# Layer 0's latent stage: its narrow transposes emitted one at a time behind every third wide matmul

## The chip, the cores and the metric

The kernel runs on one core of a Trainium2 chip. The metric is the device time of one execution in microseconds (us); the time of a kernel is the median of its runs.

TensorE (PE in the profile) multiplies matrices and also transposes 128x128 blocks, as a product with an identity matrix; VectorE (DVE), ScalarE (ACT) and GpSimd (POOL) do the elementwise work; SyncE (SP) issues most DMA transfers. Each engine takes its instructions in the order of its own queue, so an instruction that waits holds up all those behind it on that engine. The order in each queue is fixed when the kernel is built: the framework schedules with a simulated timeline and keeps the order edges that the program adds.

## The reference, cut to what matters

A two-layer backbone over 2048 latent rows and 256 context rows of width 1024. Layer 0 (even) computes, from the modulated rows `h`, query and key/value latents, the heads of a latent attention, and the inputs of a gated linear attention:

```python
h = rms_norm(x, norm_g[i]) * (1 + scale) + shift
lat = split_cols(jnp.dot(h, w_in), EVEN_SPLITS)          # lat[0]: 768, lat[1]: 256, lat[2]: 32 columns
...
q = jnp.dot(rms_norm(q_lat, q_norm), w_uq).reshape(bsz, n, A_HEADS, A_QK)
kv = jnp.dot(rms_norm(kv_lat, kv_norm), w_ukv).reshape(bsz, n, A_HEADS, A_NOPE + A_V)
k = jnp.concatenate(
    [kv[..., :A_NOPE], jnp.broadcast_to(k_rope[:, :, None, :], (bsz, n, A_HEADS, A_ROPE))], axis=-1)
q = rms_norm(q, q_gain)
k = rms_norm(k, k_gain)
...
q = jnp.concatenate([q[..., :A_NOPE], apply_axial_rope(q[..., A_NOPE:], cos, sin)], axis=-1)
```

Everything is float32. The kernel splits each factor of a product into a high and a low half and sums three products (high x high, high x low, low x high). The latent stage makes q, k and v of all rows and writes them to DRAM; the attention that follows reads them back.

## The kernel before

The stage is `even_latent` (lines 393 to 590). Its 2304 rows are 18 tiles of 128 (`NT` is 18; tiles 0 and 1 are context). For each tile:

1. *Rows.* `prep` (line 314) loads the tile from DRAM into `x`, which has one buffer (line 322). ACT squares it with an accumulated sum, `rpow` makes the factor `ssx`, and DVE scales `x` in place (line 328). TensorE transposes it in 8 blocks (line 331) into two PSUM buffers `px` of four blocks each. `modulate` then has ACT apply scale and shift from `modA` and `modB` back into `x`, and splits the result into the halves `hhi` and `hlo` (two buffers each); the modulated rows are stored to `H` by a DMA that ACT issues.
2. *Row products.* `gemm` multiplies them with the weights W0, W1, W2 of 352 columns each, 24 products a weight (8 blocks of depth, three half-products each), 72 in all, in the PSUM tiles `gm`. ACT copies each result into the latent tile `u`; `scaled` normalizes it.
3. *Latents.* `up` (line 487) transposes `u` in 8 blocks into two PSUM tiles `tp` (line 495), splits them into `lth` (ACT) and `ltl` (DVE, line 498), one buffer each, and multiplies: 36 query products of 384 columns with `WU`, into `up` tiles, then 12 key/value products of 512 columns with `wkv`. The values go through `vn` (one buffer) to DRAM. Then come the norms and the rotary embedding that make `qn` and `kn`.
4. *Heads.* `fin` (line 541) transposes the queries and then the keys, 8 heads each, in four groups of four into `tp` tiles (line 549). ACT and DVE scale and split each group into `qkhl` (two buffers, line 553), and SP stores it to `QT` or `KT`.

So a tile has 120 wide products and 32 transposes. `px`, `tp`, `gm` and `up` have two PSUM buffers each, all eight banks. The modulation of later layers (`ada_steps`) is spread over the loop: its scale-and-shift rows end in small transposes that also take `tp` buffers.

The loop (lines 571 to 590) runs steps `s` from 0 to 19. Step `s` emits, in this order: the rows of tile `s+1`, the row products of tile `s`, one step of the modulation, `up` of tile `s-1`, `fin` of tile `s-2`. In each of these the transposes are emitted in one go, 8, or 4 and 4, and the scheduler may move them against products that do not depend on them. From step 17 on, `rest_steps` loads and splits further weights (`w_rest`), and `first` (line 559) computes the last two tiles' row products with two of them, in steps 18 and 19; its result passes through the buffer of `vn`. All three-fold products go through `mm3` (line 114). Every ACT operation has line 106, that of the helper `act`.

The next stage begins with the products `mx` (line 651), which read back the stored queries as `mq` and the keys as `mk`.

Of the kernel before, what the change touches and what calls it, by code (L numbers as in the profile page):

```python
# [10 lines left out]
F32 = mybir.dt.float32  # L11
F32R = mybir.dt.float32r
AF = mybir.ActivationFunctionType
ALU = mybir.AluOpType
# [74 lines left out]
class Kern:  # L89
    def __init__(self, tc, nc, ins, scr):  # L90
        self.tc, self.nc, self.i, self.scr = tc, nc, ins, scr
        self.n = 0
        self.ahead, self.calls, self.chain = [], 0, None

# [19 lines left out]
    def mm3(self, out, lhs, rhs, ks, start=True, stop=True):  # L114

        lh, ll = lhs
        rh, rl = rhs
        n = len(ks)
        for j, k in enumerate(ks):
            self.nc.tensor.matmul(out, lh(k), rh(k), start=start and j == 0, stop=False)  # L120
            self.nc.tensor.matmul(out, lh(k), rl(k), start=False, stop=False)
            self.nc.tensor.matmul(out, ll(k), rh(k), start=False, stop=stop and j == n - 1)

    def mm3_steps(self, out, lhs, rhs, ks):
        lh, ll = lhs
        rh, rl = rhs
        n = len(ks)
        for j, k in enumerate(ks):
            self.nc.tensor.matmul(out, lh(k), rh(k), start=j == 0, stop=False)  # L129
            self.nc.tensor.matmul(out, lh(k), rl(k), start=False, stop=False)  # L130
            yield self.nc.tensor.matmul(out, ll(k), rh(k), start=False, stop=j == n - 1)  # L131
# [185 lines left out]

    def transposed(self, t, src, pp, tag, xp=None):

        nc, sp = self.nc, self.prp  # L320
        x = self.tl(xp or sp, [P, D], "x", bufs=1)
        self.xload = nc.sync.dma_start(x[:], src[t * P : t * P + P, :])
        hi = self.tl(sp, [P, KD, P], "hhi", F32R, bufs=self.hbufs)
        lo = self.tl(sp, [P, KD, P], "hlo", F32R, bufs=self.hbufs)
        ss = self.tl(sp, [P, 2], "ssx")
        self.act(lo[:].rearrange("p k t -> p (k t)"), x[:], AF.Square, accum_out=ss[:, 0:1])
        self.rpow(ss[:, 1:2], ss[:, 0:1], 1.0 / D, EPS)
        nc.vector.tensor_scalar(out=x[:], in0=x[:], scalar1=ss[:, 1:2], scalar2=None, op0=ALU.mult)
        ps = [self.tl(pp, [P, 4, P], tag[0], bufs=tag[1]) for _ in range(2)]
        for k in range(KD):  # L330
            nc.tensor.transpose(ps[k // 4][:, k % 4, :], x[:, k * P : k * P + P], self.ident[:])
        return x, ps, hi, lo
# [60 lines left out]
    def even_latent(self, ws, wrest, kept):  # L393
# [5 lines left out]
        with ExitStack() as es:  # L399
# [87 lines left out]
            def up(t):  # L487
                u, ss = lat.pop(t)
                lh = self.tl(sp, [P, 8, P], "lth", F32R, bufs=1)
                ll = self.tl(sp, [P, 8, P], "ltl", F32R, bufs=1)  # L490
                for g in range(2):
                    ps = self.tl(pp, [P, 4, P], "tp")
                    for j in range(4):
                        k = g * 4 + j
                        nc.tensor.transpose(ps[:, j, :], u[:, k * P : k * P + P], self.ident[:])
                    s = slice(g * 4, g * 4 + 4)
                    self.act(lh[:, s, :], ps[:])
                    nc.vector.tensor_tensor(out=ll[:, s, :], in0=ps[:], in1=lh[:, s, :], op=ALU.subtract)
# [43 lines left out]
            def fin(t):  # L542
                qn, kn = nat.pop(t)
                for z, (src, dst) in enumerate(((qn, self.QT), (kn, self.KT))):
                    col = 2 * z + (0 if t < NCT else 1)
                    for h2 in range(2):
                        ps = self.tl(pp, [P, 4, P], "tp")
                        for j in range(4):
                            nc.tensor.transpose(ps[:A_QK, j, :], src[:, h2 * 4 + j, :], self.ident[:])
                        hl = self.tl(sp, [P, 4, 2, P], "qkhl", F32R, bufs=2)  # L550
                        hi, lo = hl[:A_QK, :, 0, :], hl[:A_QK, :, 1, :]
                        self.act(hi, ps[:A_QK], AF.Copy, scale=qkg[:A_QK, col : col + 1])
                        nc.vector.scalar_tensor_tensor(out=lo, in0=ps[:A_QK], scalar=qkg[:A_QK, col : col + 1],
                                                       in1=hi, op0=ALU.mult, op1=ALU.subtract)
                        nc.sync.dma_start(
                            dst[h2 * 4 : h2 * 4 + 4, :, :A_QK, t * P : t * P + P].rearrange("h s d t -> d (h s) t"),
                            hl[:A_QK].rearrange("d h s t -> d (h s) t").bitcast(F32))
# [12 lines left out]
            ahead = (_ for j in (2, 3, 4) for _ in self.rest_steps(wrest, j, ws, f"W{j - 2}"))  # L570
            for s in range(NT + 2):
# [1121 lines left out]
```

## Time and profile before

| | |
|---|---|
| median of 3 runs | 3750.93 us (3749.34 to 3751.32) |
| the profiled execution | span 3751.7 us |
| mean granted TensorE clock over the span | 0.973 |
| latent stage, first W1 product to first `mx` | 45.2 to 568.4 us |
| wide and narrow products of TensorE in this stretch | 2880 |
| DMA in this stretch | 82.7 MB, mean 158 GB/s |

The whole span, cut into the start, the latent stage, and three stretches of what follows (the attention, the gated linear attention, and the rest with layer 1), shows where the work lies. Columns: the stretch, busy time and count of each engine (PEld is TensorE's weight load, which overlaps its products), TensorE's granted clock as a share of full speed, the mean busy share of the 16 DMA engines, and their rate.

```profile
core 0: us, PE busy (x) PEld busy (x) DVE busy (x) ACT busy (x) POOL busy (x), PEclk, DMA share, GB/s
0.00:45.20 45.20, 33.05 (x160) 20.79 (x160) 14.31 (x29) 18.55 (x36) 3.86 (x17) 0.92 0.82 310
45.20:568.40 523.20, 489.37 (x2880) 452.64 (x2880) 348.33 (x634) 263.13 (x608) 180.90 (x326) 0.96 0.54 158
568.40:1000.00 431.60, 429.76 (x2212) 379.41 (x2213) 351.43 (x591) 59.35 (x103) 42.44 (x73) 1.00 0.26 81
1000.00:1700.00 700.00, 690.56 (x3471) 458.80 (x3469) 503.43 (x735) 337.67 (x665) 135.86 (x136) 0.99 0.32 90
1700.00:3751.00 2051.00, 1944.33 (x9686) 1460.76 (x9684) 1158.22 (x2873) 759.14 (x1329) 843.72 (x784) 0.97 0.54 155
```

How to read the lines of the next part: a row of the timeline gives start, busy time, engine and line, operation, out<-in by the program's names, the shapes, and the count of like instructions run together; in square brackets stands the wait ahead of it and what ended it. Instructions overlap in TensorE's pipeline, so the time from one start to the next (a slot) is what a product costs, not its busy time.

### The profile page before, as it was taken

The page shows a single profiled execution, that of the slowest core. Times are in us where ns is not written, and L with a number is a line of the kernel's source. Part 1 is how long each engine was busy: PE and PEld are TensorE (multiplying, and loading weights), DVE is VectorE, ACT ScalarE, POOL GpSimd, SP SyncE. Part 2 cuts the span into 40 slices and gives each one's busy share as a digit, 9 for nine tenths or more (in the row PEclk, how much of TensorE's full clock was granted, in tenths as well). Part 3 has the DMA queues.
Part 4 walks back from the last instruction along what each step waited for, and adds up shares of the span by engine and source line. Part 5 has one row for each costly group of instructions (what it writes and reads, how often), then busy time and mean ns, then how long its engine had stood idle before and what let it go on. Part 6 is the DMA issues. An engine that isn't in the chain of part 4 may idle for free.

```text
span 3751.7 us, 51747 instructions
## 1 busy us (share of the span) xinstructions
PE 3587.1 (96%) x18404; PEld 2772.4 (74%) x18404; DVE 2375.7 (63%) x4860; ACT 1437.8 (38%) x2741; POOL 1206.8 (32%) x1336
## 2 busy tenths in 40 slices
PE   7999989999999999999999999999899999898889
PEld 6988988888886666656657878887688886555567
DVE  4677656888866666696754344455578774666722
ACT  4445541111125555545552134444222224444400
POOL 1434320010111222212202233333444435776643
PEclk9999999999999999999999999999999999999899
DMA  7455453222252231425515545545544448777464
GB/s 254 138 161 162 130 168 96 80 81 80 77 134 66 75 108 57 117 82 149 143 37 180 162 141 155 148 146 166 178 138 147 127 114 225 188 183 201 140 194 131
DMA packets 364371, 512.18 MB, mean 137 GB/s; under 512 B 25825, under 2 KB 243889, under 8 KB 358210
## 3 DMA queue, kind: packets, MB, share of 16 engines
q1 hardware_dynamic: 322642, 425.49, 39.5%
q0 software_dynamic: 19872, 55.92, 4.9%
q10 hardware_dynamic: 21600, 27.46, 2.1%
q8 instruction: 146, 2.39, 0.3%
q14 instruction: 111, 0.91, 0.1%
HBM read 329.38 MB, written 179.37 MB: 136 GB/s over the span
## 4 chain that ended last, share of the span: by engine, by line
PE 78%; DVE 8%; DMA 6%; POOL 4%; ACT 3%; issue 2%; SPq 0%; POOLq 0%; DVEq 0%; ACTq 0%
PE gm L129 9%; PE gm L130 9%; PE gm L131 9%; PE av L905 7%; PE st L963 4%; PE mx L651 4%; PE st L964 3%; PE st L965 3%; PE pj L129 3%; PE pj L130 3%; PE pj L131 3%; POOL oacc L1409 2%; PE o L1403 1%; DMA wraw<-w_od 1%; PE st L1373 1%
## 5 line engine op out<-in xcount | busy, mean ns | idle before, releaser
L954 DVE TENSOR_TENSOR acc<-acc,apt 128x512 f32<-128x512 f32 x512 | 364.6, 737 | 155.3 <-ACT apt L106 152.3
L106 ACT ACTIVATE apt<-st 128x512 f32<-128x512 f32 (+1 forms) x592 | 343.9, 593 | 282.5 <-PE st L965 245.3
L652 DVE TENSOR_REDUCE mm<-mx 128x1 f32<-128x512 f32 (+1 forms) x656 | 389.2, 629 | 82.1 <-PE mx L651 75.1
L905 PE MATMUL av<-apt,av 128*64 128x512 f32 (+1 forms) x1184 | 286.2, 597 | 0.0
L963 PE MATMUL st<-aq,akh 97*128 97x512 f32 (+1 forms) x592 | 254.0, 429 | 5.8 <-ACT apt L106 3.0
L1409 POOL TENSOR_TENSOR oacc<-oacc,opt 128x576 f32<-128x576 f32 (+6 forms) x192 | 221.4, 1178 | 87.0 <-ACT opt L106 85.3
L651 PE MATMUL mx<-mk,mq 96*128 96x512 f32 (+1 forms) x656 | 236.8, 373 | 6.1 <-DMA mq<-QT 4.7
L964 PE MATMUL st<-aq,akh 96*128 96x512 f32 (+1 forms) x592 | 235.1, 397 | 0.0
L965 PE MATMUL st<-aq,akl 96*128 96x512 f32 (+1 forms) x592 | 234.0, 396 | 0.0
L1286 DVE CUSTOM_DVE_ANT_1 mx<-mx,mtab 128x225 f32<-128x225 f32 (+12 forms) x576 | 183.8, 339 | 61.4 <-PE mx L1280 45.9
L106 ACT ACTIVATE u<-gm 128x352 f32<-128x352 f32 (+1 forms) x140 | 68.5, 497 | 369.8 <-PE gm L131 208.8
L905 PEld LDWEIGHTS av<-apt,av 128*64 128x64 f32 x1184 | 81.6, 137 | 155.3 <-issue 154.1
L1531 DVE TENSOR_TENSOR opt<-st,tab 128x64 f32<-128x64 f32 (+10 forms) x576 | 142.5, 314 | 78.7 <-PE st L1374 50.8
L963 PEld LDWEIGHTS st<-aq,akh 97*128 97x128 f32 x592 | 112.4, 190 | 98.9 <-issue 43.7
L1073 POOL TENSOR_TENSOR px<-py,px 128x512 f32<-128x512 f32 x64 | 86.2, 1348 | 231.5 <-DVE py L1072 220.4
L106 ACT ACTIVATE opt<-opt 128x930 f32<-128x930 f32 (+8 forms) x130 | 104.4, 805 | 138.1 <-DVE opt L1531 129.3
L1373 PE MATMUL st<-q,kt 128*128 128x480 f32 (+5 forms) x256 | 104.3, 409 | 47.2 <-DVE opt L1531 42.5
L651 PEld LDWEIGHTS mx<-mk,mq 96*128 96x128 f32 x656 | 121.7, 189 | 17.7 <-issue 5.1
L106 ACT ACTIVATE prh<-pr 128x1024 fp32r<-128x1024 f32 x32 | 33.9, 1058 | 263.4 <-PE pj L130 235.7
L965 PEld LDWEIGHTS st<-aq,akl 96*128 96x128 f32 x592 | 113.5, 192 | 25.5
L964 PEld LDWEIGHTS st<-aq,akh 96*128 96x128 f32 x592 | 114.1, 193 | 18.0
L106 ACT ACTIVATE x<-px,modB,modA 128x128 f32<-128x128 f32 x272 | 99.1, 468 | 57.9 <-DVE onat L1139 27.6
(513 smaller groups left out, 10054.6 us busy)
## 6 DMA issues: line engine op xcount, KB each, us to landing
q<-Q SPq DMA_DIRECT2D x48, 512.0 KB
H<-x ACTq DMA_DIRECT2D x36, 512.0 KB
adaw<-ada_w SPq DMA_DIRECT2D x64, 256.0 KB
x<-H SPq DMA_DIRECT2D x32, 512.0 KB
pr<-RT SPq DMA_DIRECT2D x32, 512.0 KB
wraw<-w_od SPq DMA_DIRECT2D x64, 256.0 KB
K1t<-okt POOLq DMA_DIRECT2D x32, 512.0 KB, 7.7
kt<-K1t SPq DMA_DIRECT2D x32, 512.0 KB
```

Source lines behind the costliest of these rows:

```text
L106: return self.nc.scalar.activation(out, in_, func, **kw)
L129: self.nc.tensor.matmul(out, lh(k), rh(k), start=j == 0, stop=False)
L130: self.nc.tensor.matmul(out, lh(k), rl(k), start=False, stop=False)
L131: yield self.nc.tensor.matmul(out, ll(k), rh(k), start=False, stop=j == n - 1)
L651: mm = nc.tensor.matmul(ps[:, :w], q[:A_QK, (t % 6) * P : (t % 6) * P + P], k[:A_QK, k0 : k0 + w], start=True, stop=True)
L652: nc.vector.tensor_reduce(out=m[:, t, n : n + 1], in_=ps[:, :w], axis=AX.X, op=ALU.max)
L905: nc.tensor.matmul(O[j, nb][i * 64 : i * 64 + 64, :w], V[j, kt // TT][:, kt % TT, i * 64 : i * 64 + 64], pts[i][:, :w], start=n == 0, stop ...
L954: nc.vector.tensor_tensor(out=acc[i][:, :w], in0=a[:, :w], in1=pts[i][:, :w], op=ALU.add)
L963: nc.tensor.matmul(ps[:, :w], kh[: A_QK + 1, i, kq], qh[: A_QK + 1, :w], start=True, stop=False)
L964: nc.tensor.matmul(ps[:, :w], kh[:A_QK, i, kq], ql[:A_QK, :w], start=False, stop=False)
L965: mm = nc.tensor.matmul(ps[:, :w], kl[:A_QK, i, kq], qh[:A_QK, :w], start=False, stop=True)
L1409: self.psum = nc.gpsimd.tensor_tensor(out=a, in0=a, in1=pts[:, :, a0 - r0 : a1 - r0, :], op=ALU.add)
```

## The change

In this stage alone, transposes are no longer emitted as a batch. Each group becomes a generator, one transpose at a time, with the work on a finished PSUM tile (modulation, split or store) emitted behind the last transpose of the group: behind the 4th of four, or, for rows, behind the 8th. `queue` puts such a generator in a list. The new `mm` emits one wide product; it then takes the first generator in the list whose count is due, emits its next transpose with an order edge behind this product, and puts an order edge from that transpose to the next wide product (`hold`). A generator is due again three wide products later. `finish_task` emits all that is left of a generator at once.

```diff
+    def queue(self, gen, wait=0, every=3):
+        task = [self.wide + wait, every, gen]
+        self.narrow.append(task)
+        return task
...
+    def finish_task(self, task):
+        if task in self.narrow:
+            self.narrow.remove(task)
+        for _ in task[2]:
+            pass
+
+    def mm(self, out, l, r, start, stop):
+        with self.tc.issue_after(self.hold.ins) if self.hold else ExitStack():
+            mm = self.nc.tensor.matmul(out, l, r, start=start, stop=stop)
+        self.hold = None
+        self.wide += 1
+        for task in self.narrow:
+            if task[0] <= self.wide:
+                with self.tc.issue_after(mm.ins):
+                    self.hold = next(task[2], None)
+                if self.hold is None:
+                    self.narrow.remove(task)
+                task[0] = self.wide + task[1]
+                break
+        return mm
...
+    def transposes(self, ps, parts, src, done):
+        for n, i in enumerate(parts):
+            t = self.nc.tensor.transpose(ps(i), src(i), self.ident[:])
+            if n == len(parts) - 1:
+                done()
+            yield t
...
+    def prep_task(self, l, t, src, pp, tag, wait):
+        x, hi, lo = self.scaled(t, src)
+        def steps():
+            ps = []
+            for g in range(2):
+                ps.append(self.tl(pp, [P, 4, P], tag[0], bufs=tag[1]))
+                done = (lambda: self.modulate(l, t, x, ps, hi, lo)) if g else lambda: None
+                yield from self.transposes(lambda k: ps[g][:, k, :], range(4), lambda k: x[:, (g * 4 + k) * P : (g * 4 + k + 1) * P], done)
+        return hi, lo, self.queue(steps(), wait)
```

`transposed` and `scaled` are the two parts of the former `transposed`. The latents' transposes leave `up` and become the generator `turn`, with the split of each four behind its fourth; `fin` becomes a generator, with the split and the store of each group behind its fourth. The loop queues the rows of tile `s+1` with a wait of 10 wide products, the latents of tile `s-1` with a wait of 40, and the queries and keys of tile `s-2` with a wait of 2, the last ahead of the products of `up(s-1)`, not behind them:

```diff
             for s in range(NT + 2):
                 if 0 < s < NT - 1:
                     with tc.issue_after(behind.ins) if s == 1 else ExitStack():
-                        hT[s + 1] = self.prep(0, s + 1, self.i["xin"], pp, px)
+                        *hT[s + 1], tasks["x", s + 1] = self.prep_task(0, s + 1, self.i["xin"], pp, px, 10)
+                if 1 < s <= NT:
+                    tasks["u", s - 1] = self.queue(turn(s - 1), 40 if s < NT else 0)
                 if s == 0:
                     gemm(0, 1)
                 elif 1 < s < NT:
+                    begin(("x", s))
                     gemm(s)
...
-                for f, d in ((up, 1), (fin, 2)):
-                    if s >= NT - 1:
-                        for _ in zip(range(3), ahead):
-                            pass
-                        if f == fin and s >= NT:
-                            first(NT - 1, s - NT + 2)
-                            first(NT - 2, s - NT + 2)
-                    if 0 <= s - d < NT:
-                        f(s - d)
+                if s >= NT - 1:
+                    for _ in zip(range(3), ahead):
+                        pass
+                if 0 <= s - 1 < NT:
+                    if s == 1:
+                        tasks["u", 0] = self.queue(turn(0))
+                    begin(("u", s - 1))
+                    if 0 <= s - 2:
+                        tasks["q", s - 2] = self.queue(fin(s - 2), 2)
+                    up(s - 1)
+                if s >= NT - 1:
+                    for _ in zip(range(3), ahead):
+                        pass
+                if s >= NT:
+                    if s > NT:
+                        tasks["q", s - 2] = self.queue(fin(s - 2), 2)
+                    first(NT - 1, s - NT + 2)
+                    first(NT - 2, s - NT + 2)
+                begin(("q", s - 2))
+            self.finish_tasks()
```

`begin` calls `finish_task` for a task that has not run dry. So what is left of the rows of tile `s` is emitted ahead of its row products, and what is left of its latents ahead of its query products. Other stages call `mm3` too; there the list is empty, and `mm` adds no order edge. The text of these stages is unchanged.

More of the change, by code (lines that the diff above doesn't have):

```diff
@@ L93, in __init__ @@
         self.ahead, self.calls, self.chain = [], 0, None
+        self.narrow, self.wide, self.hold = [], 0, None
     def pool(self, es, name, bufs=1, space=None, **kw):
@@ L112, in load, with finish_tasks, mm3 @@
         return self.chain
[L114 to L122, printed above, removed]
+    def queue(self, gen, wait=0, every=3):
+        task = [self.wide + wait, every, gen]
+        self.narrow.append(task)
+        return task
+    def finish_tasks(self):
+        while self.narrow:
+            self.finish_task(self.narrow[0])
+    def finish_task(self, task):
[17 more added lines that the diff above has]
+        return mm
+    def mm3(self, *a):
+        for _ in self.mm3_steps(*a):
+            pass
     def mm3_steps(self, out, lhs, rhs, ks):
@@ L328, in transposed @@
         nc.vector.tensor_scalar(out=x[:], in0=x[:], scalar1=ss[:, 1:2], scalar2=None, op0=ALU.mult)
[L329 to L332, printed above, removed]
+        return x, hi, lo
     def modulate(self, l, t, x, ps, hi, lo):
```

53 lines of the change are left out of this document (33 added, 20 removed).

## Prediction

> **What bounds the kernel now.** I read the page first, then the busy time by stretch of layer 0's latent stage, which the change is confined to, then TensorE's waits in each stretch, then single instructions.
>
> ```profile
> span 3751.7 us, 51747 instructions
> ...
> PE 3587.1 (96%) x18404; PEld 2772.4 (74%) x18404; DVE 2375.7 (63%) x4860; ACT 1437.8 (38%) x2741; POOL 1206.8 (32%) x1336
> ```
>
> TensorE is busy 96% of the span, so what the kernel can gain by a new order is what TensorE loses. The stage runs from the first W1 product at 45.2 us to the first product of the next stage at 568.4. I cut it into a head (tiles 0 to 2), sixteen regular tiles, and a tail after the last tile's row product:
>
> ```profile
> core 0: us, PE busy (x) PEld busy (x) DVE busy (x) ACT busy (x) POOL busy (x), PEclk, DMA share, GB/s
> 45.20:100.00 54.80, 47.19 (x252) 44.73 (x253) 34.82 (x53) 28.00 (x62) 11.79 (x19) 0.88 0.62 194
> 100.00:491.50 391.50, 383.51 (x2309) 353.60 (x2308) 275.97 (x519) 204.98 (x493) 150.94 (x282) 0.99 0.51 149
> 491.50:568.40 76.90, 58.66 (x323) 54.31 (x321) 37.54 (x64) 30.14 (x53) 18.17 (x27) 0.89 0.64 181
> ```
>
> TensorE's loss is its idle time and its time at a lowered clock (1 minus PEclk, times the length). Head: 7.6 + 6.6 = 14.2 us. Middle: 8.0 + 3.9 = 11.9. Tail: 18.2 + 8.5 = 26.7. Together 53 us, 1.4% of the span: no order of the same instructions gains more here. The waits behind the idle time, in the same three stretches:
>
> ```profile
> PE px L331 <- DVE x L328: 2.7, 1, 2.7
> PE up L122 <- DVE ltl L498: 2.7, 1, 2.7
> PE up L120 <- ACT lth L106: 1.1, 1, 1.1
> ```
> ```profile
> PE up L122 <- DVE ltl L498: 3.8, 5, 1.7
> PE tp L495 <- DVE modA L302: 1.9, 1, 1.9
> PE tp L549 <- DVE qkhl L553: 1.5, 2, 1.2
> PE px L331 <- DVE x L328: 0.4, 1, 0.4
> ```
> ```profile
> PE gm L120 <- ACT vn L106: 5.9, 1, 5.9
> PE mx L651 <- DMA mq<-QT: 4.7, 1, 4.7
> PE tp L495 <- DVE qkhl L553: 4.4, 2, 3.5
> ```
>
> Each row is total, times, longest. The middle is nearly tight: five waits for the low half of the latents (ltl) are half of its idle time. Head and tail hold the large ones.
>
> **The change part by part.** No instruction is added or removed: the same 16,410 TensorE instructions, 560 of them transposes of this stage, and the same DMAs, in another order. 534 transposes now stand alone between wide products. *Price of a single.* Four in a batch, and one alone:
>
> ```profile
> 139.06 0.32 PE L121 MATMUL gm<-W0l,hhi 128*128 128x352 f32 x1
> 139.22 0.60 PE L549 MATMUL tp<-ident,kn 128*96 128x128 f32 x4
> 139.58 0.41 PE L122 MATMUL gm<-W0h,hlo 128*128 128x352 f32 x1
> 139.82 0.32 PE L120 MATMUL gm<-W0h,hhi 128*128 128x352 f32 x1
> ```
> ```profile
> 246.20 0.34 PE L121 MATMUL up<-WUl,lth 128*128 128x384 f32 x1
> 246.38 0.27 PE L549 MATMUL tp<-ident,qn 128*96 128x128 f32 x1
> 246.41 0.42 PE L122 MATMUL up<-WUh,ltl 128*128 128x384 f32 x1
> 246.67 0.34 PE L120 MATMUL up<-WUh,lth 128*128 128x384 f32 x1
> ```
>
> A row product takes a slot of 0.16 (139.06 to 139.22), a query product 0.18. From 139.06 to 139.82 are 0.76 us; less two slots, four transposes cost 0.44, 0.11 each. The single: 0.47 less two slots of 0.176 is 0.12, equal within the rounding. So standing alone saves nothing and costs 0 to 0.01 each, 0 to +5 us over 534; I take a quarter of that, **+1.3**, since both figures round to 0.11 or 0.12.
>
> The Trainium skill (TensorE: Matmul & The Clock Gate, "Back-to-back issue gap") gives an isolated 128-column matmul 56 ns once warm, and says that weight loads are pulled ahead of running matmuls; by it a single between wide products might cost half of 0.11. The single above does not show it; it is a rival below.
>
> *Head.* Now tile 0's latents are transposed at once behind the W2 products, tile 2's rows singly among tile 0's query products, and tile 3's rows follow after 5 query, 11 row and 12 key products. With a key slot of 0.24,
>
> ```profile
> 136.04 0.40 PE L120 MATMUL up<-wkvh,lth 128*128 128x512 f32 x1
> 136.28 0.39 PE L121 MATMUL up<-wkvl,lth 128*128 128x512 f32 x1
> ```
>
> that is 0.9 + 1.8 + 2.8 = 5.5 us of cover. The rows' tile x has one buffer: modulation must end before the next load, and square, power and scale follow it. Before, that chain took
>
> ```profile
> 63.75 1.97 PE L331 MATMUL px<-ident,x 128*128 128x128 f32 x8 [2.74 <-DVE x L328]
> 65.95 1.97 PE L495 MATMUL tp<-ident,u 128*128 128x128 f32 x8 [0.23 <-DVE u L467]
> ```
> ```profile
> 79.14 0.74 DVE L328 TENSOR_SCALAR x<-x,ssx 128x1024 f32<-128x1024 f32 x1
> ```
> ```profile
> 85.79 1.50 ACT L106 ACTIVATE x<-px,modB,modA 128x128 f32<-128x128 f32 x4 [2.41 <-DMA wraw<-w_rest]
> ```
>
> from 65.7 to 79.9, 14.2 us. With singles the first four modulations (1.5 us) and their split lie ahead of the last transpose, so 1.5 to 2.6 come off: 11.6 to 12.7, against 5.5. A wait of 6 to 7 us for x stands in TensorE's queue with everything behind it, and SP now issues this x load behind two loads of rest weights, up to 2 us more. I take 7, and 2.5 for the clock (waits of 7.6 in this stretch cost 6.6 at lowered clock before). Gone: the two waits for lth and ltl, 3.8, and their clock, about 1.7. Tile 2's eight transposes lay in the wait up to 65.95, which stays, and now take 1.0 of busy time. Head: 7 + 2.5 - 5.5 + 1 = **+5**, bounds 0 (x lands early) to +9.
>
> *Middle.* The latents are now transposed some 40 wide products into the next row product, so at least 11 row products lie between the last of them and the first query product: I take the ltl waits (3.8) as gone, half of the other 4.2 of the 8.0 idle, since the scale-and-shift rows and the q and k groups still share two PSUM buffers, and half of the clock loss, 2: -7.9, bounds 0 and -11.9. New: the row chain. Eight row transposes are now spread over 7 to 10 us, and from the last of a tile to the first of the next there are 16.0 to 18.2 us of slots at nine tiles, 13.4 at two, 22 at two. The chain took, at two tiles where the next transposes followed on its heels,
>
> ```profile
> 162.58 1.04 PE L331 MATMUL px<-ident,x 128*128 128x128 f32 x8
> 188.45 0.49 PE L331 MATMUL px<-ident,x 128*128 128x128 f32 x3
> ```
> ```profile
> 180.31 0.76 DVE L328 TENSOR_SCALAR x<-x,ssx 128x1024 f32<-128x1024 f32 x1 [1.32 <-POOL ssx L202]
> 208.69 0.75 DVE L328 TENSOR_SCALAR x<-x,ssx 128x1024 f32<-128x1024 f32 x1 [0.60 <-POOL ssx L202]
> ```
>
> 17.5 and 20.5 us from the last transpose to the scaled rows; less 2.6 it is 15 to 18. I take the nearer, the first: only the two tiles with 13.4 wait, 1.7 each, **+3.4**; bounds 0 and +20 (first rival).
>
> *Tail.* Tile 17's queries are transposed after tile 17's 12 key products and only 4 row products of the rest weights, 4 us of slots; before, 48 row products lay between. But they cannot start earlier than they are ready:
>
> ```profile
> 525.78 0.49 ACT L106 ACTIVATE qn<-up 128x384 f32<-128x384 f32 x1 [0.22 <-PE up L122]
> 537.82 0.46 ACT L106 ACTIVATE vn<-gm 128x352 f32<-128x352 f32 x1
> ```
> ```profile
> 540.90 0.42 DVE L485 TENSOR_TENSOR qn<-rx,rrot 128x256 f32<-128x256 f32 x1
> 551.18 1.21 PE L549 MATMUL tp<-ident,kn 128*96 128x128 f32 x8 [1.21 <-DVE qkhl L553]
> ```
>
> From the last query product (525.8) to the last key transpose (552.1) are 26.3 us, 12 of them until the copy vn frees PSUM for the row products, 15.5 until tile 17's queries are ready (541.3). Now it is the longer of the two, 12 to 15.5, plus 44 row products and 16 singles, 8.8: 21 to 24.3, a gain of 2 to 5.3. The last four groups are spread over those 9 us, so the last copy need no longer wait for the store of the first queries, as it did:
>
> ```profile
> 556.64 0.75 DVE L553 SCALAR_TENSOR_TENSOR qkhl<-tp,qkg,qkhl 96x512 fp32r<-96x512 f32 x1 [0.43 <-ACT qkhl L106]
> 568.38 0.55 PE L651 MATMUL mx<-mk,mq 96*128 96x256 f32 x1 [4.72 <-DMA mq<-QT]
> ```
>
> The last split ended 5.2 us after the last transpose; at 0.69 + 0.75 plus queueing it would be about 2.5, so the 4.7 us wait of the next stage loses some 2.5. Ahead of it, tile 16's queries come after 8 us of slots against a like chain (a new wait of some 3), in place of the 4.4 waited for qkhl: 1 off. Tail: -3.5 - 2.5 - 1 with the clock, which follows the idle time, -1, and half of it held back because ACT and SP carry the rest weights here: **-6**, bounds +2 and -12.
>
> Sum: +1.3 + 5 - 7.9 + 3.4 - 6 = -4.2 on the profiled 3751.7, which lies 0.8 above the median 3750.93: 3746.7, **3747 us**. Later stages carry the same work in a slightly changed order on a TensorE that idles little there; I give them 3 us either way.
>
> **Rivals.** *The row chain becomes the clock of the tile (slower).* Place: the first row transpose of tiles 5 to 17, with TensorE's whole queue behind it. It decides once the chain, less the overlap, exceeds 16.2 us; at 18.2 the shortfalls over the slots are 2, 2, 1.8, 4.8, 4.8, 0.7, 2.2, 1.8 and small ones, 20 us, in place of +3.4: 3747 + 17, and the middle's gain of 7.9 shrinks by a third as tiles are already stalled: **3767**. For it: one of the two rows above gives 18, and SP's queue has the next x load behind the last key store of the tile two back, which comes later than before. Against: the other gives 15, and in the whole middle TensorE waited 0.4 us for x.
> *All of the middle's waits go, and x3 lands early:* head 0, middle -11.9 + 1.3, tail -7: **3733**. For it: every tile now has the same order, and ltl, half the waits, has cover. Against: DVE, which is late in all of the middle's rows shown, has as much to do as before.
> *A single costs only its stream.* If its load and that of the product behind it hid, it would take 128/352 of 0.16, 0.058: 0.052 saved 534 times is 28: **3720**. Against: the single at 246.38.
>
> **How the numbers follow.** The sum 0.50 (3747, own range 3739 to 3756), the row chain 0.21, all waits gone 0.20, cheap singles 0.04, later stages worse by 10 to 15 us, 3760, 0.05 (nothing in the profile speaks for it but that their order changes too). A measurement of this kernel tells 0.2%, 7.5 us, from no change. Of the sum's 0.50, 0.11 falls below 3743.4 and 0.02 above 3758.4; so faster 0.35, the same 0.37, slower 0.28. The range 3731 to 3769 takes in the second rival and the row chain's price, and leaves out cheap singles.
>
> **What would show it.** Singles: the slot between wide products around a lone transpose stays at 0.11 to 0.12 above them. Head: a wait of about 7 us of px for x near 85, and none for ltl. Middle: ltl gone from TensorE's waits, idle below 8 us; many waits of px for x of 1 to 5 us mean the first rival. Tail: the wait for vn or the queries near 8 to 10, that for mq near 2. Wrong is the forecast if the middle's idle time exceeds 15 us or the head's loss stays under 14.

## The result, and the profile after

The changed kernel is slower: 3756.31 us (median of 19 runs, 3752.3 to 3763.61) against 3746.57 us before (19 runs, 3743.28 to 3751.32), a ratio of 1.0027 with a 95% interval of 1.002 to 1.0033. That is +9.7 us. The profiled executions hide it: the span of the profile of before (3751.7) is longer than any of its 19 runs, and the profiled run of the changed kernel (3752.8, span 3751.0) is among the shortest of its own. From the page of the changed kernel's profile:

```profile
span 3751.0 us, 51768 instructions
...
PE 3576.3 (95%) x18404; PEld 2751.3 (73%) x18404; DVE 2377.5 (63%) x4860; ACT 1438.8 (38%) x2741; POOL 1199.2 (32%) x1336
```

The latent stage alone tells another story. It took 523.1 us before (45.2 to 568.4) and 541.4 (44.9 to 586.3) after. The busy time by stretch, cut where the same work ends (head to the end of tile 3's W2 products, middle to the end of tile 17's, tail to the first `mx`):

```profile
core 0: us, PE busy (x) PEld busy (x) DVE busy (x) ACT busy (x) POOL busy (x), PEclk, DMA share, GB/s
44.90:135.30 90.40, 71.71 (x400) 66.31 (x400) 48.39 (x73) 43.67 (x99) 21.38 (x38) 0.89 0.51 156
135.30:507.40 372.10, 362.20 (x2170) 319.68 (x2170) 264.81 (x500) 192.90 (x456) 138.47 (x263) 1.00 0.51 148
507.40:586.40 79.00, 59.46 (x314) 52.51 (x313) 37.16 (x62) 30.34 (x53) 17.50 (x26) 0.83 0.61 174
```

TensorE is idle for 18.7 us in the head and 19.5 in the tail. The larger of its waits, for head, middle and tail in turn (total, times, longest):

```profile
PE px L163 <- DVE x L384: 8.8, 1, 8.8
PE gm L134 <- ACT u L107: 6.0, 3, 5.2
PE tp L163 <- DVE u L520: 4.4, 1, 4.4
```
```profile
PE tp L163 <- DVE qkhl L612: 5.6, 7, 2.0
PE tp L332 <- DVE adab L327: 1.6, 1, 1.6
PE up L134 <- ACT qn L107: 1.3, 2, 0.7
PE px L163 <- DVE x L384: 1.0, 1, 1.0
```
```profile
PE gm L134 <- ACT vn L107: 13.1, 2, 8.9
PE up L134 <- ACT lth L107: 2.3, 1, 2.3
PE tp L163 <- DVE qn L538: 2.3, 1, 2.3
PE mx L731 <- DMA mq<-QT: 1.1, 1, 1.1
```

The waits for `ltl` are gone everywhere. In their place stand a long one for `x`, a new one of a row product for ACT's copy to `u`, one of 4.4 us of tile 0's latent transposes for `u` (0.2 before), seven short ones of latent transposes for the split of queries and keys, and 13.1 us for `vn`.

To compare stretches in which the work is ordered differently, I give each TensorE instruction of the stage its slot (0.16 us a row product, 0.1755 a query product, 0.2335 a key/value product, 0.11 a transpose, and so on). These slots add up to 467.4 us in every kernel here, as all run the same TensorE instructions between the first W1 product and the first `mx`. What a stretch takes beyond its slots is its loss: idle time, products at a lowered clock, and slots that run over (in the middle of the changed kernel only 9.9 of the 19.3 us are idle, at a mean clock of 1.00). The prediction added idle time and all the time at a lowered clock, which counts idle time at a lowered clock twice: its tail lost 26.7, here it is 24.9. The "later part" runs from the first `mx` to the end of the span. All figures are us of one profile each; the ratios are of timed runs and hold the later part too, so a ratio alone does not tell what the stage did.

| kernel | loss head | middle | tail | stage | later part | ratio to before (95%) |
|---|---|---|---|---|---|---|
| before, two profiles | 14.5; 14.6 | 16.4; 15.1 | 24.9; 24.5 | 523.1; 521.6 | 3183.3; 3179.5 | 1 |
| changed, two profiles | 26.9; 28.4 | 19.3; 27.1 | 27.8; 26.9 | 541.4; 549.8 | 3164.7; 3168.1 | 1.0027 (1.002 to 1.0033) |
| e1 own copy buffers | 28.1 | 19.6 | 23.9 | 539.1 | 3168.7 | 1.0036 (1.0023 to 1.0048) |
| e2 rows batched | 22.7 | 28.1 | 28.4 | 546.7 | 3167.9 | 1.0049 (1.0035 to 1.0063) |
| e3 latents batched | 12.0 | 20.3 | 28.6 | 528.4 | 3165.5 | 0.9993 (0.9983 to 1.0002) |
| e4 heads batched | 18.9 | 22.1 | 21.7 | 530.1 | 3173.7 | 1.0018 (1.0009 to 1.0027) |
| e7 context key copied | 20.0 | 19.6 | 25.8 | 532.9 | 3164.6 | 1.0005 (0.9996 to 1.0013) |
| e8 latents batched, old tail | 15.5 | 19.1 | 21.9 | 523.9 | 3171.6 | 0.9977 (0.9968 to 0.9985) |
| e9 no order edges | 15.4 | 10.5 | 15.6 | 508.9 | 3164.9 | 0.9948 (0.9936 to 0.9961) |
| e10 every product | 10.3 | 11.4 | 24.6 | 513.7 | 3176.4 | 0.9979 (0.997 to 0.9988) |
| e11 rows alone | 15.1 | 34.5 | 22.3 | 539.4 | 3177.5 | 1.0065 (1.005 to 1.0079) |
| e12 one edge | 18.2 | 12.0 | 16.6 | 514.2 | 3171.2 | 0.9964 (0.9952 to 0.9976) |
| e13 heads later | 22.3 | 51.3 | 22.0 | 563.1 | 3172.1 | 1.0076 (1.0061 to 1.009) |

### The profile page after: what moved, and what is told of

It reads as the page before. It is cut to its first block, busy times and chain, and to the rows that moved or that the text cites. A ratio compares the mean times of both kernels' runs of the same rounds, so it can differ in the third digit from the quotient of the medians.

```text
span 3751.0 us, 51768 instructions
## 1 busy us (share of the span) xinstructions
PE 3576.3 (95%) x18404; PEld 2751.3 (73%) x18404; DVE 2377.5 (63%) x4860; ACT 1438.8 (38%) x2741; POOL 1199.2 (32%) x1336
## 4 chain that ended last, share of the span: by engine, by line
PE 76%; DVE 7%; DMA 7%; POOL 4%; ACT 3%; issue 3%; SPq 0%; POOLq 0%; DVEq 0%; ACTq 0%
PE gm L134 29%; PE pj L134 9%; PE av L985 7%; PE st L1043 4%; PE mx L731 4%; PE st L1045 3%; PE st L1044 3%; PE o L1483 2%; PE up L134 2%; PE st L1453 2%; DMA adaw<-ada_w 1%; DMA wraw<-w_od 1%; PE o L1465 1%; DVE oacc L1473 1%; PE st L1454 1%
## 5 line engine op out<-in xcount | busy, mean ns | idle before, releaser
L1034 DVE TENSOR_TENSOR acc<-acc,apt 128x512 f32<-128x512 f32 x512 | 375.3, 755 | 170.0 <-ACT apt L107 167.0
L1366 DVE CUSTOM_DVE_ANT_1 mx<-mx,mtab 128x225 f32<-128x225 f32 (+13 forms) x576 | 184.1, 339 | 62.5 <-PE mx L1360 42.7
L731 PEld LDWEIGHTS mx<-mk,mq 96*128 96x128 f32 x656 | 121.3, 188 | 13.1 <-DMA mk<-KT 1.5
```

The costliest lines, as they stand in the source:

```text
L731: mm = nc.tensor.matmul(ps[:, :w], q[:A_QK, (t % 6) * P : (t % 6) * P + P], k[:A_QK, k0 : k0 + w], start=True, stop=True)
L1034: nc.vector.tensor_tensor(out=acc[i][:, :w], in0=a[:, :w], in1=pts[i][:, :w], op=ALU.add)
L1366: nc.vector.tensor_tensor_reduce(out=s, in0=s, in1=tb[:, ri : ri + rn, ci : ci + cn], scale=1.0, scalar=-3e38, op0=ALU.add, op1=ALU.max, a ...
```

## The experiments

### The same two kernels again

**e5.** The kernel before, no edit.

> The kernel before, unchanged, profiled a second time. The part from the first mx to the end took 3183 us in its first profile and 3155 to 3165 in the changed kernel and the four kernels so far, while the medians of whole runs differ by 10 us at most and the latent stage alone by 5 to 24. Theory: the first profile of the kernel before caught a long execution of the later stages (its run, 3751.3, was the longest of those known then); a second one gives a stage of 523 within 1 us and a later part of 3170 to 3175. Rival: the later part is slower by its order, then it is 3180 or more again.

Stage 521.6, later part 3179.5 (3747.8 less 568.3): the stage repeats within 1.5 us, the later part stays long. That is the rival to within 0.5 us; the theory's 3170 to 3175 did not come. **e6.** The changed kernel, no edit.

> The changed kernel, unchanged, profiled a second time: stage 541.4 within 2 us, later part between the first profile's 3164.7 and 3172. Rival: the stage itself scatters by more than 3 us from run to run, and then single profiles of the experiments cannot be compared to that accuracy.

Later part 3168.1, as expected, but stage 549.8: there the rival held. The stage of one and the same program scattered by 8 us, nearly all in the middle (19.3 and 27.1); this second execution, 3766.2 us, is longer than all 19 runs given above. So a difference of less than about 8 us between the stages of two fixed-order kernels tells nothing by itself; waits that come and go with an edit, and the ratios, do.

By the means of the two profiles the stage costs 23 us more (545.6 against 522.4) and the later part 15 less (3166.4 against 3181.4). Together +8, against the +9.7 measured. The text of the later stages is the same in both kernels, but not the order that the scheduler made of them: of the 16,410 instructions in TensorE's program, only the last 919 stand in the same order as before. The changed kernel, e2, e3 and e7 have the last 13,629 in common, and their five profiles give 3164.6 to 3168.1 there. So the gain goes with the order. That the order is its cause is argued, not shown: it was not tried to give the kernel before that order alone.

### One kind of transpose at a time

**e2.** Rows in a batch:

```diff
-                        *hT[s + 1], tasks["x", s + 1] = self.prep_task(0, s + 1, self.i["xin"], pp, px, 10)
+                        hT[s + 1] = self.prep(0, s + 1, self.i["xin"], pp, px)
```

> The changed kernel with the row transposes in a batch, as before; latents, queries and keys stay single. Theory: only the head gains. Tile 2's rows are transposed and modulated at once, so that the wait for x of tile 3 (8.8 us) falls to 3 to 5 us; the middle is within 2 us of the changed kernel, because TensorE waits there for x only 1.0 us in all. Stage 541.4 to about 536. Rival (the spread row chain costs in many tiles): the middle loses 8 us or more of its idle time, stage 530 or below.

Neither came: stage 546.7, slower than before by 0.49%. The wait for `x` went (2.5 us left), but an 11.8 us wait of a row product for ACT's copy to `u` took its place, and the waits for `qkhl` in the middle rose to 17.2 us. The stage lies within the scatter of the changed kernel's own. **e3.** Latents in a batch:

```diff
-                if 1 < s <= NT:
-                    tasks["u", s - 1] = self.queue(turn(s - 1), 40 if s < NT else 0)
...
-                    if s == 1:
-                        tasks["u", 0] = self.queue(turn(0))
-                    begin(("u", s - 1))
+                    self.finish_task(self.queue(turn(s - 1)))
```

> The changed kernel with the latent transposes in a batch ahead of the query products, as before; rows, queries and keys stay single. Theory: the waits of latent transposes for the split of queries and keys (qkhl, 5.6 us in seven waits) go, and waits of query products for the low half of the latents (ltl) of about 4 us come back: stage within 3 us of 541.4. Rival (the early latents are what holds up the copies to u and the heads): stage below 535. Other rival (early latents are the gain of the change): stage above 546.

Stage 528.4: the first rival held, and my theory (within 3 us of 541.4) fell, though the waits changed as it said (none for `qkhl` in the middle, 2.2 us for `ltl`). The gain lies in the head, whose loss fell from 26.9 to 12.0. With no latents tied into tile 2's row products, tile 1's query products run ahead of tile 3's rows: the first of these stands at 90.5 us, with no wait for `x`, where the changed kernel stood idle from 80 to 89. **e4.** Queries and keys in a batch behind the products of `up`:

```diff
-                    if 0 <= s - 2:
-                        tasks["q", s - 2] = self.queue(fin(s - 2), 2)
...
-                    if s > NT:
-                        tasks["q", s - 2] = self.queue(fin(s - 2), 2)
...
-                begin(("q", s - 2))
+                if 0 <= s - 2:
+                    self.finish_task(self.queue(fin(s - 2)))
```

> The changed kernel with queries and keys transposed in a batch behind the key/value products of the next tile, as before; rows and latents stay single. Theory: the tail's extra loss is the emission of tile 16's queries and keys among tile 17's query products, where they wait for qn and qkhl and put off tile 17's values, whose store holds up the copy; undone, the waits for qn (2.3) and 7 of the 13.1 us for vn go, and the middle's qkhl waits fall by half: stage 541.4 to about 531. Rival: the heads are not what costs, stage within 3 us of 541.

Stage 530.1 as the theory had it, and the tail as it said: the wait for `vn` fell from 13.1 to 6.2 us, the loss of the tail from 27.8 to 21.7. But the theory's sum was right by luck: the middle's waits for `qkhl` rose to 10.3 us instead of falling by half, and the head, of which the theory said nothing, lost 8.0 us less (18.9 for 26.9). **e11.** Only rows single (e3's and e4's edits together):

> Only the rows are emitted singly in a fixed order; latents, queries and keys are batched as before. Theory: the row chain costs nothing, as its waits for x are at most 1.6 us in the middle of any run so far: stage 521 to 526, later part 3154 to 3172 as the scheduler happens to order it, kernel 3735 to 3748. Rival (rows spread over 7 to 10 us delay the chain): waits for x of 5 us and more in the middle, stage 530 or above.

The row chain did cost nothing (0.4 us of waits for `x` in the middle), yet the middle lost 34.5 us, more than with all four kinds. The largest of TensorE's waits there:

```profile
PE up L134 <- ACT lth L107: 6.4, 6, 2.1
PE tp L332 <- DVE adab L327: 4.6, 2, 3.1
PE up L134 <- DVE ltl L552: 3.1, 3, 1.7
```

Query products wait for latents just transposed, as before, but now, as I read it, the row products that could fill these waits are tied to row transposes. That was not tested, and it leaves out 8.8 us of waits of transposes for the modulation's rows (`adab`, `modA` and `modB`). Neither theory nor rival had the reason. Undoing the kinds one by one does not add up (e3 and e4 gain, both together lose), which spoke against a price per kind and for something that all share.

### The order itself

**e9.** The same generators, places and loop, without the two order edges:

```diff
-        with self.tc.issue_after(self.hold.ins) if self.hold else ExitStack():
-            mm = self.nc.tensor.matmul(out, l, r, start=start, stop=stop)
+        mm = self.nc.tensor.matmul(out, l, r, start=start, stop=stop)
...
-                with self.tc.issue_after(mm.ins):
-                    self.hold = next(task[2], None)
+                self.hold = next(task[2], None)
```

> The changed kernel's emission (generators behind every third wide product, the same waits and the same loop), but without the order edges between wide products and transposes, so that the scheduler may move them. Theory: what costs is the fixed order, in which TensorE cannot put other products into a wait: the head's 9 us for x and the waits in tile 3's row products shrink, stage 541 to 550 falls to about 530; the tail, which depends on the emission, keeps its 13 us for vn. Rival: the emission itself (late values, buffers held longer by spread groups) costs, the stage stays above 538.

Stage 508.9, 32 us below the changed kernel's shorter one and 13 below the kernel before; 0.52% faster than before, of which, by the profiles, less than half is the stage's and the rest the later part's (3164.9). Against the changed kernel all three stretches gained; against the kernel before the head did not (15.4 for 14.5). Its windows, cut at the same work:

```profile
45.50:124.40 78.90, 70.73 (x399) 66.68 (x400) 47.95 (x73) 42.45 (x99) 23.26 (x38) 0.91 0.55 174
124.40:487.70 363.30, 358.36 (x2170) 325.22 (x2169) 262.54 (x501) 192.68 (x456) 151.42 (x264) 1.00 0.52 152
487.70:554.50 66.80, 54.12 (x315) 50.41 (x313) 36.69 (x61) 30.81 (x53) 16.36 (x24) 0.91 0.73 210
```

The middle idles 4.9 us of 363, and its waits are of two kinds:

```profile
PE tp L161 <- DVE qkhl L610: 2.9, 5, 1.0
PE tp L161 <- DVE modA L335: 1.9, 1, 1.9
```

In the trace 248 transposes still stand alone between wide products (530 in the changed kernel); the scheduler put the others together again. The tail, which I had not expected to gain, waits for `vn` once (7.9 us), not twice. **e12.** Only the edge from a transpose to the next wide product is taken away (the first two lines removed in the diff of e9):

> The changed kernel without the second of its two order edges: a transpose still stands behind its wide product, but the next wide product is no longer tied behind the transpose. Theory: the costly part is that all products queue behind a transpose that is late; with that edge gone the stage comes within 3 us of the run without order edges (508.9), and the head's wait for x is below 4. Rival: the edge that places the transpose is the one that costs (a transpose may not stand earlier or later than its third product), the stage stays above 525.

Stage 514.2, 0.36% faster than before; the wait for `x` in the head is 3.6 us, the middle waits 4.4 us for `qkhl`. The theory held but for its margin (5 us above e9, not 3). Most of the price, 27 of 32 us, is this one edge: every following product queues behind a transpose that is late. The later part is 3 to 7 us longer than in the changed kernel, so the gain over that kernel is the stage's. But here too the scheduler put about half of the transposes together again (285 stand alone). **e10.** A transpose behind every product, with both edges:

```diff
-    def queue(self, gen, wait=0, every=3):
+    def queue(self, gen, wait=0, every=1):
```

> The changed kernel with a transpose behind every wide product, not every third, in the same fixed order. Theory: a group of four holds its PSUM buffer for 4 slots less (0.9 instead of 2.3 us), so the waits of latent transposes for the split of queries and keys (5.6 and 7.9 us in the two profiles) fall below 3; head and tail stay: stage 535 to 540. Rival (these waits come from DVE, which is late whenever the transposes stand): they stay at 5 or more and the stage at 541 to 550.

Better than expected, stage 513.7, and 0.21% faster than before with both edges in place. The waits for `qkhl` fell to 1.6 us in the middle, as the theory said, and the head's wait for `x` went altogether. That fewer products are tied while something is late, as the generators are done sooner, would explain both; it was not tested apart. The tail kept 14.9 us for `vn`. **e13.** Queries and keys further back, both edges kept:

```diff
-                        tasks["q", s - 2] = self.queue(fin(s - 2), 2)
+                        tasks["q", s - 2] = self.queue(fin(s - 2), 26 if s < NT else 2)
```

> The changed kernel with both edges, but queries and keys start 26 wide products into the query products of the next tile, not 2, except in the last two steps; they then stand 104 to 122 products behind the products that make them (77 on average in the changed kernel, about 103 without edges). Part of the latents' transposes falls out of the spread order by this. Theory: in the fixed order the nearer queries and keys are what makes latent transposes wait for qkhl in the middle (5.6 and 7.9 us); these waits go and the middle's loss falls from 19 to 27 us to about 14; the head's wait for x and the tail stay; stage about 530. Rival: the middle's loss comes from the fixed order as such, and the stage stays at 540 or above.

The theory fell; it is the slowest of all, stage 563.1. In the middle:

```profile
PE tp L163 <- DVE qkhl L612: 26.6, 15, 2.9
PE gm L134 <- ACT u L107: 3.0, 6, 0.9
```

It was not the distance to the products that make them. Moved back, the last groups of keys run into the next tile's latents; these rows are transposes waiting for a `tp` buffer whose group is not yet split, and with the fixed order no other product comes ahead of them. The rival had the direction; that the loss would grow to 51 us it did not say.

### Two waits by themselves

**e7.** The two context tiles' unrotated key columns are copied out of `u`:

```diff
-                if t >= NCT:
-                    kb = self.tl(sp, [P, 1, 32], "kbase")
+                kb = self.tl(sp, [P, 1, 32], "kbase")
+                if t < NCT:
+                    nc.gpsimd.tensor_copy(kb[:, 0, :], kr)
+                    kr = kb[:, 0, :]
+                if t >= NCT:
```

> The changed kernel, but for the two context tiles the unrotated 32 key columns are first copied out of u by GpSimd, as the rotary embedding does for the other tiles, so that u comes free before the key norms. Theory: the 5.2 us wait of TensorE for a gm buffer in tile 3's row products goes (ACT's copy to u waits there for GpSimd's last read of tile 1's u), with 1.5 us of half clock behind it: stage 541.4 to about 535, kernel 6 us below the changed one. Rival: GpSimd is held by the key norms at that place too, so the copy comes no earlier and the stage stays within 2 us.

The 5.2 us wait for the copy to `u` went, and with it 7 to 8 us of the head's loss (26.9 and 28.4 to 20.0). The head's waits are then:

```profile
PE px L163 <- DVE x L384: 9.2, 1, 9.2
PE tp L163 <- DVE u L520: 5.1, 1, 5.1
```

The kernel came 2.6 us above the before of its own chip (3751.66 against 3749.11), a ratio whose interval takes in 1. **e1.** The copy of the rest-weight row products gets other buffers:

```diff
-                u = self.tl(sp, [P, LAT_CHUNK], "vn", bufs=1)
+                u = self.tl(sp, [P, LAT_COLS], "u", bufs=2)[:, :LAT_CHUNK]
```

> The changed kernel, except that the copy of the rest-weight row products goes through the two buffers of u, which are idle by then, and no longer through the one buffer of vn. Theory: in the changed kernel TensorE waits twice for that copy (8.9 and 4.2 us), because it waits for the store of tile 17's values and then for its own store. Both waits go; the next to be late are tile 17's queries, ready 12 us after the last key/value product with 8 us of row products ahead of them, so a wait of about 4 us appears for qn. Stage from the first W1 product to the first mx: 541.4 to about 531 us, kernel about 10 us below the changed one. Rival: the queries and their stores set the end anyway, then the stage stays within 2 us of 541.

The waits for `vn` went and the tail lost 3 to 4 us less (23.9), but the stage stayed at 539.1 and the ratio at 1.0036: the rival. In the tail TensorE waits instead for tile 17's queries:

```profile
PE tp L163 <- DVE qn L538: 15.0, 2, 12.8
```

I had put 4 us there. **e8.** e3's edits, and in the last two steps queries and keys in a batch behind the products:

> The changed kernel with the latents in a batch (as in the run with latents batched, stage 528.4) and, in the last two steps alone, queries and keys in a batch behind the products, as before. Theory: the two gains add, the tail loses some 5 us less (before 24.9 us, latents batched 28.6): stage about 524, kernel about 4 us below the run with latents batched, 3739 to 3741, below the kernel before. Rival: the tail is set by DVE and the stores in any order, and the stage stays at 527 to 530.

Stage 523.9: the two gains add, as the theory said. But the stage is no shorter than before (521.6 and 523.1); that the kernel is 0.23% faster than before comes with the later part, 3171.6 against 3179.5 and 3183.3.

## Why the prediction was wrong

The forecast was 3747, 0.1% faster. The time of 3756.3 lies within its range, but the kernel is 0.27% slower, and by none of the ways that the rivals gave. That the time lies in the range is no merit: the range is 38 us wide, and the forecast was counted from a median of 3 runs that lies 4.4 us above that of 19. Nor would its own signs have shown the error: the middle's idle time is 9.9 us (wrong above 15) and the head's loss 26.9 (wrong under 14). By its steps, with the losses of the two profiles of the changed kernel less 14.5, 15.8 and 24.7, the means of before:

**Price of a single, +1.3: right.** Three row products and a transpose among them in the changed kernel:

```profile
330.37 0.41 PE L134 MATMUL gm<-W0l,hhi 128*128 128x352 f32 x1
330.61 0.32 PE L134 MATMUL gm<-W0h,hlo 128*128 128x352 f32 x1
330.77 0.32 PE L134 MATMUL gm<-W0h,hhi 128*128 128x352 f32 x1
330.93 0.27 PE L163 MATMUL px<-ident,x 128*128 128x128 f32 x1
330.96 0.41 PE L134 MATMUL gm<-W0l,hhi 128*128 128x352 f32 x1
```

From 330.37 to 330.96 are 0.59 us; less three slots of 0.16 it is 0.11. Over the 530 that stand alone the median is 0.114, against 0.110 each in a batch of four before: 534 times 0.004 is 2 us. Cheap singles did not come: the trace, not the 56 ns gap that the Trainium skill (TensorE: Matmul & The Clock Gate, "Back-to-back issue gap") gives for an isolated 128-column matmul, was the one to go by, with 0.11 in both.

**Head, +5 (bounds 0 and +9): too small, +12 and +14.** The wait for `x` was forecast at 7 and is 8.8. The term was right in its place and 2 us short. The chain from the end of the last row transpose (74.8) to the scaled rows (89.0) is 14.2 us, as long as before, where I had taken 1.5 to 2.6 off:

```profile
74.52 0.27 PE L163 MATMUL px<-ident,x 128*128 128x128 f32 x1
```
```profile
88.28 0.74 DVE L384 TENSOR_SCALAR x<-x,ssx 128x1024 f32<-128x1024 f32 x1
```

The overlap itself came: the last modulation ended 1.8 us behind that transpose, at 76.6, where in the kernel before it had ended 4.3 us behind it. The gain was lost again behind the modulation. SP's next load waits for the store of the modulated rows to `H`. It was issued 3.8 us after that store (first pair), and 2.7 us after it in the kernel before (second pair):

```profile
76.64 0.33 ACTq L398 DMA_DIRECT2D H<-x  x1
80.45 0.33 SPq L378 DMA_DIRECT2D x<-xin  x1
```
```profile
70.06 0.33 ACTq L345 DMA_DIRECT2D H<-x  x1
72.75 0.33 SPq L322 DMA_DIRECT2D x<-xin  x1
```

Why the store took longer was not tested. From the issue of the load to ACT's square it took 0.4 us more, and from the square to the scaled rows 1.0 more, as GpSimd scaled keys (`kn`) between the two operations that make the factor. The cover was as forecast: TensorE reached the transpose 5.3 us behind the row at 74.5, at 79.8. The wait of some 2.9 us ahead of the first transposes, which was to stay, became 4.4, for `u`. What the step left out altogether is the wait of tile 3's row products for ACT's copy to `u`. The chain in the changed kernel:

```profile
126.43 1.12 POOL L596 TENSOR_TENSOR kn<-u,sqk 128x256 f32<-128x256 f32 x1
127.58 0.82 ACT L107 ACTIVATE u<-gm 128x352 f32<-128x352 f32 x2 [5.48 <-POOL kn L596]
128.10 0.66 PE L134 MATMUL gm<-W2h,hhi 128*128 128x352 f32 x1 [5.20 <-ACT u L107]
```

`u` has two buffers. Tile 3's first copy needs that of tile 1, a context tile, whose last reader is GpSimd's key scaling, the end of the chain of tile 1's norms. Before, the same wait of ACT was longer and cost TensorE nothing, as transposes and query products stood behind it:

```profile
99.96 1.12 POOL L537 TENSOR_TENSOR kn<-u,sqk 128x256 f32<-128x256 f32 x1
101.11 0.82 ACT L106 ACTIVATE u<-gm 128x352 f32<-128x352 f32 x2 [9.86 <-POOL kn L537]
```

e7 confirms it by its removal. I had costed the head by the buffers of `x` alone and not looked for who else holds a buffer that two tiles share.

**Middle, -7.9 + 3.4: wrong in sign, +3.5 and +11.** Some 1.7 of it is the price of the 428 singles that stand there. The `ltl` waits went, as forecast. The row chain's 3.4 (3.0 by its own rows: 17.5 less 2.6 less 13.4, twice) is 1.0. But "half of the other 4.2" became more: the waits for `qkhl` alone are 5.6 (7.6 in the second profile). The failed step is the silent one under all terms, that a wait costs its own length less its cover, in an order where the cover can be named. The fixed order has as much cover on paper, but when a transpose is late, the products that the scheduler would run first are tied behind it. e9 and e12 show that the edge is what costs at this spacing: the same emission without it brings the middle to 10.5 and 12.0, below the kernel before. What stays open is how much of that comes from the transposes which the scheduler then put together again; and e10, with both edges and a spacing of one, has a middle of 11.4, so it is the edges and the spacing together that cost.

**Tail, -6 (bounds +2 and -12): wrong in sign, +3 and +2.** The -6 does not follow from its terms as written: they add up to -8, and half of that is -4, by which the forecast would have been 3749. Of the +3 some 1.3 is idle time (19.5 for 18.2); the granted clock was 0.83 for 0.89. I took the end to follow the longer of two chains, 12 us to the copy `vn` or 15.5 to tile 17's queries. The first wait for `vn` is indeed 12.8 us behind the last query product (543.9 to 556.7). But the copy then waits once more, for its own store, and both waits stand on TensorE's path:

```profile
551.51 0.49 SPq L576 DMA_DIRECT2D Vn<-vn  x1
```
```profile
556.23 0.46 ACT L107 ACTIVATE vn<-gm 128x352 f32<-128x352 f32 x1 [0.76 <-DMA Vn<-vn]
561.34 0.46 ACT L107 ACTIVATE vn<-gm 128x352 f32<-128x352 f32 x1 [4.66 <-DMA Un<-vn]
```
```profile
556.74 0.66 PE L134 MATMUL gm<-W1h,hhi 128*128 128x352 f32 x1 [8.92 <-ACT vn L107]
561.86 0.66 PE L134 MATMUL gm<-W1h,hhi 128*128 128x352 f32 x1 [4.16 <-ACT vn L107]
```

From the last query product to the last key transpose (573.6) are 29.7 us, where I had 21 to 24.3. The second copy was left out; before, it had its 5.4 us (ACT's wait for the store of `Un`) beside products not tied to anything. e1 shows that the buffer is not the whole cause either: without its waits the queries are late by as much. e4 and e8 show that the old emission of the last heads wins back 5 to 7 us. The wait for `mq` fell from 4.7 to 1.1, a gain of 3.6 for a forecast 2.5.

**Later stages, 3 us either way: wrong, -15.** The scheduler's order of the later stages changed with the stage, to the better, and the 15 us that came with it hide two thirds of the stage's loss. The rival of later stages 10 to 15 us worse had the reason, their changed order, and the wrong sign. By the means of the profiles the stage alone, 23 us, would be 0.6%.

**Rivals.** The row chain as the clock of the tile: no, 1.0 us of waits for `x` in the middle of either profile. All the middle's waits gone: not here; e9 comes near it (4.9 us idle), with an order left to the scheduler and fewer than half of the transposes alone, so that is not a gain of singles as such. Singles that cost their stream alone: no.

## What to carry to other kernels

An order edge costs nothing as long as nothing is late; when something is, it costs every instruction behind it that could have run. Before fixing an order by hand, count what a scheduler would have had to fill each wait with, and fix only the place of the narrow instruction, not what follows it: here, with a transpose behind every third product, that one edge is the difference between a kernel 0.4% faster than before (e12, half of it in the later stages) and one 0.3% slower. The edges are not bad at any spacing: e10 keeps both, behind every product, and is 0.2% faster than before. And profile twice: the same program's stage scattered by 8 us, and an edit in one stage moved the order of stages whose text it did not touch, and 15 us with it.

## What the runs showed of the hardware that was not expected

One transpose that waits for nothing costs 0.114 us between wide products and 0.110 in a batch: breaking up batches is nearly free on TensorE here.

The granted clock can fall behind a short wait. In the changed kernel TensorE waited 1.6 us until 222.4 (for `adab`), and the clock was 0.50 from 223.1 to 226.4; yet a wait of 2.0 us that ended at 214.1 lowered nothing, so the length of a wait alone does not decide. In the tail, with waits of 2.3, 0.8 and 2.3 us, the clock was 0.50 from 530.3 to 540.5, and query products took slots of 0.32 us there, not 0.18.
